# A hybrid decoder layer on one core: FFN's first tile with VectorE in program order, row scaling as a step of its own, block differences ahead of low parts

## The chip, the cores and the metric

The kernel runs on one core of a Trainium2 chip. The metric is the device time of one execution in microseconds (us), as the median of several runs. A profile of one more execution was taken; its times are counted from the start of its span.

## The reference, cut to what matters

The layer is `h = h + mixer(h)`, `h = h + cross_attention(h)`, `h = h + conv_glu(rmsnorm(h))`, with 1024 rows of 1024 columns. The change lies where the second line ends and the third begins:

```python
def conv_glu(hn, w_ffn_in, conv_w, conv_b, w_ffn_out):
    a, gate = jnp.split(hn @ w_ffn_in, 2, axis=-1)          # D_FF = 2816 columns each
    conv = conv_b + sum(a_pad[:, j:j + S] * conv_w[j] for j in range(3))
    return (jax.nn.gelu(conv) * gate) @ w_ffn_out
# hn = h * rsqrt(mean(h * h) + EPS) * g_ffn, row by row
```

## The kernel before, in words

Every f32 operand of a product is kept as a high and a low part (`xh`, `xl` or two halves of a page `wp`), and `mm3` (L308 to L311) makes each product of three matmuls. ScalarE (ACT) or GpSimd (POOL) rounds the high part, VectorE (DVE) or POOL subtracts for the low part.

**Rows.** The 1024 rows are eight groups `t` of 128, here called rows. `xo_unit(c, t)` computes half `c` of the output of cross attention for row `t`: 24 matmuls into one of two `acc` banks, then one addition on DVE (L1300) into `h2[t]`. After the second half, `f_norm(t)` stores `h2[t]` (a DMA issued by ACT, L1307), squares and sums it on ACT (L1135), makes the reciprocal root with two small DVE instructions (L133, L134) and ten small ACT instructions (L137), and scales the row with two DVE instructions of 128x512 (L1315), in place for rows 4 to 7. `f_tr(t)` transposes the scaled row on TensorE (PE, eight 128x128 transposes, L1381, into the two `trp` banks).

**The seven products.** `ffn_in(f)` computes one of 22 column tiles of the first FFN product for all rows with seven block products instead of eight (Strassen's scheme in Winograd's form): the operands are the blocks B11, B21, B22 and the sums T1 to T4 of the rows, and sums of the weights. For rows 0 to 3 `f_tr` splits the transposed row into B11 and B21 (ACT casts L1332, DVE low parts L1335). For rows 4 to 7 it makes B22 in the same way, x11 and x21 (L1346, on DVE and POOL), T1 = block - x11 (L1394, DVE), T2 = block - T1 (L1396, DVE), and with T2 on POOL T3 (L1398) and T4 (L1400). `xb_finish` splits each T of all four rows into high (ACT, L1360) and low parts (DVE, L1361). `product` issues 12 matmuls into one of six PSUM banks; DVE adds up the seven results (L1455). Then come the convolution (ACT L1496, DVE L1497 and L1498), the gelu (ACT L1499) and the gate (POOL L1504).

**Weights.** A queue of jobs loads and splits the weight pages. For each tile f there are the jobs A (2 pages), S (three DVE sums, L225 to L227), B (2 pages and the DVE difference L233), C (2 pages) and D (1 page). A page costs an ACT cast (L201) and a DVE subtraction (L204). `W.pump(1)` emits the next job if no more than 12 pages would be in use; a product gives its page back. The raw weights come by SP's queue into two buffers of 512 KB; a load is issued when the subtraction that read the buffer last is done.

**Order.** The program is traced once; a scheduler orders each engine's instructions from a model of their times. In the block `manual_schedule` (L1605 to L1618) PE keeps program order. Instructions of the program behind the block (tiles f = 1 to 21) may stand among those of the block on every engine.

Of the kernel before, what the change touches and what calls it, by code (L numbers as in the profile page):

```python
# [21 lines left out]
NT = 8  # L22
# [22 lines left out]
def hybrid_layer(ctx, tc, I, out):  # L45
# [28 lines left out]
    def trp():  # L74
        return ps.tile([P, 512], F32, name=nm("trp"), tag="tr", bufs=2)

    def accp():
        return ps.tile([P, 512], F32, name=nm("acc"), tag="acc", bufs=2)

    def small(name, shape=(P, 8), bufs=8):  # L80
        return wpool.tile(list(shape), F32, name=nm(name), tag=name, bufs=bufs)
# [47 lines left out]
    def rstd1(r, ss, scale):  # L129

        w = small("rst", (P, 3, 8), 4)
        m, y, t, u = (w[:, 0, j:j + 1] for j in range(4))
        dve.tensor_scalar(m, ss, scale, EPS, op0=OP.mult, op1=OP.add)  # L133
        dve.tensor_scalar(y.bitcast(I32), m.bitcast(I32), -0.5, 1597463007.0, op0=OP.mult, op1=OP.add)  # L134

        def mul(o, x, f, bias=0.0):
            act.activation(o, x, AF.Copy, bias=bias, scale=f)  # L137
        mul(t, y, y)
        mul(t, t, m)
        mul(t, t, -3.0 / 16, 9.0 / 16)  # L140
        mul(y, y, t)
        mul(t, y, y)
        mul(t, t, m)
        mul(u, t, 64.0 / 9, -10.0 / 3)
        mul(t, t, u)
        mul(t, t, 64.0 / 9, 5.0)
        mul(r, t, y)
# [16 lines left out]
    class Weights:  # L164
# [27 lines left out]
        def page(self, key):  # L192
            pg = wp()
            self.used += 1
            self.pages.setdefault(key, []).append(pg)
            return pg
# [79 lines left out]
    W = Weights()  # L276
# [31 lines left out]
    def mm3(o, lh, ll, rh, rl, start, stop):  # L308
        pe.matmul(o, lhsT=lh, rhs=rh, start=start, stop=False)  # L309
        pe.matmul(o, lhsT=lh, rhs=rl, start=False, stop=False)  # L310
        pe.matmul(o, lhsT=ll, rhs=rh, start=False, stop=stop)  # L311
# [782 lines left out]
    for s in range(-2, NA + 3):  # L1094
# [21 lines left out]
        u = s - 2  # L1116
# [16 lines left out]
    def norm_rows(src, jk, ssq, r):  # L1133

        act.activation(jk, src, AF.Square, accum_out=ssq)  # L1135
        rstd1(r, ssq, 1.0 / D)
# [47 lines left out]
    def w2(shape, dt, name):  # L1184
        return w2_at[0].tile(shape, dt, name=nm(name), tag="w2", bufs=w2_at[1])
# [101 lines left out]
    hf, hst = {}, {}  # L1287

    def xo_unit(c, t, mid=None):
        pages = W.get(("xo", c), 8)  # L1290
        half, u = divmod(t, 4)
        p = accp()
        for k in range(KT):
            oh, ol = ox[k // 4, (k % 4) // 2, half]
            s = slice(u * P, (u + 1) * P)
            if k == 4 and mid:
                mid()
            mm3(p, oh[:, k % 2, s], ol[:, k % 2, s], pages[k][:, 0, :], pages[k][:, 1, :], k == 0, k == KT - 1)
        hs = h2[t][:, c * 512:(c + 1) * 512]
        dve.tensor_tensor(hs, p, hs, op=OP.add)  # L1300
        if t == NT - 1:
            W.free(8)
        W.pump(1)

    def f_norm(t):
        rs = slice(t * P, (t + 1) * P)
        act.dma_start(h2_d[rs, :], h2[t])  # L1307
        st = small("st", (P, 12), 6)
        ws = [w2([P, 512], F32, "hn") for _ in range(1 if t >= 4 else 2)]
        norm_rows(h2[t], ws[0].bitcast(BF), st[:, 0:1], st[:, 1:2])  # L1310
        hn = []
        for g in range(2):
            hg = h2[t][:, g * 512:(g + 1) * 512]
            w = hg if t >= 4 else ws[g]
            dve.scalar_tensor_tensor(w, hg, st[:, 1:2], gff[g], op0=OP.mult, op1=OP.mult)  # L1315
            hn.append(w)
        hst[t] = hn
# [5 lines left out]
    def xb_new(name):  # L1323
        XB[name] = [[page([P, 2, 512], F32R, name) for _ in range(2)] for _ in range(2)]

    def xb_put(name, u, src, eh, el):
        ss = slice(u * P, (u + 1) * P)
        for v in range(2):
            hh, ll = (XB[name][i][v][:, :, ss] for i in range(2))
            x = src[:, 256 * v:256 * v + 256].rearrange("p (k q) -> p k q", k=2)  # L1330
            if eh == "a":
                act.copy(hh, x)  # L1332
            else:
                pool.tensor_scalar(hh, x, 1.0, 1.0, op0=OP.mult, op1=OP.mult)
            (dve if el == "d" else pool).tensor_tensor(ll, x, hh.bitcast(F32), op=OP.subtract)  # L1335

    def two(ap):
        return ap.rearrange("p (k q) -> p k q", k=2)

    def xb_sum(name, u, eng):  # L1340

        w = w2([P, 512], F32, "xf")
        ss = slice(u * P, (u + 1) * P)
        for v in range(2):
            hh, ll = (XB[name][i][v][:, :, ss].bitcast(F32) for i in range(2))
            eng.tensor_tensor(two(w[:, 256 * v:256 * v + 256]), hh, ll, op=OP.add)  # L1346
        return w

    def xb_finish(name):

        if name == "T4":
            xb_new(name)
            for u in range(4):
                xb_put(name, u, t4s[u], "a", "d")
            return
        XB[name] = [[], []]
        for v in range(2):
            f = tf[name][v]
            hh, ll = (page([P, 2, 512], F32R, name) for _ in range(2))
            act.copy(hh, f)  # L1360
            dve.tensor_tensor(ll, f, hh.bitcast(F32), op=OP.subtract)  # L1361
            XB[name][0].append(hh)
            XB[name][1].append(ll)
# [3 lines left out]
    def f_tr(t):  # L1367
        half, u = divmod(t, 4)
        if t == 0:
            xb_new("B11")  # L1370
            xb_new("B21")
        if t == 4:
            xb_new("B22")
            for n in ("T1", "T2", "T3"):
                tf[n] = [page([P, 2, 512], F32, n) for _ in range(2)]
        hn = hst.pop(t)
        ps_ = []
        for g in range(2):
            p = trp()
            for j in range(4):  # L1380
                pe.transpose(p[:, j * P:(j + 1) * P], hn[g][:, j * P:(j + 1) * P], ident)  # L1381
            ps_.append(p)
            if half == 0:
                xb_put(("B11", "B21")[g], u, p, "a", "d")
        if half == 0:
            return
        x11, x21 = xb_sum("B11", u, dve), xb_sum("B21", u, pool)
        ss = slice(u * P, (u + 1) * P)
        t1, t2, t3 = ([tf[n][v][:, :, ss] for v in range(2)] for n in ("T1", "T2", "T3"))
        t4s.append(x21)  # L1390
        vs = [slice(0, 256), slice(256, 512)]
        xb_put("B22", u, ps_[1], "a", "d")
        for v in range(2):
            dve.tensor_tensor(t1[v], two(ps_[0][:, vs[v]]), two(x11[:, vs[v]]), op=OP.subtract)  # L1394
        for v in range(2):
            dve.tensor_tensor(t2[v], two(ps_[1][:, vs[v]]), t1[v], op=OP.subtract)  # L1396
        for v in range(2):
            pool.tensor_tensor(t3[v], t2[v], two(x11[:, vs[v]]), op=OP.subtract)  # L1398
        for v in range(2):
            pool.tensor_tensor(two(x21[:, vs[v]]), two(x21[:, vs[v]]), t2[v], op=OP.subtract)  # L1400

    NU = 16
    for s in range(NU + 4):
        if s < NU:
            if s + 1 < NT:
                x_tr(s + 1, page)
            x_q(s)
            W.pump(1)
            if s == 1:
                x_kv()  # L1410
        if 0 <= s - 1 < NU:
            x_qt(s - 1)
        if 0 <= s - 2 < NU:
            x_s(s - 2)
        if 0 <= s - 3 < NU:
            x_pt(s - 3)
        if s + 3 < NT:
            x_norm(s + 3, w2([P, D], BF, "jk"))
        if s >= 4 and (s - 4) % 4 == 3:
            x_o((s - 4) // 8, ((s - 4) // 4) % 2)  # L1420
        if s >= NU - 1:
            for t in range(2 * (s - NU + 1), min(NT, 2 * (s - NU + 2))):
                h2.append((page if t < 4 else kq)([P, D], F32, "h2"))
                sp.dma_start(h2[t], h_d[t * P:(t + 1) * P, :])
        if s >= NU:
            xo_unit(0, s - NU)
        W.pump(1)
# [5 lines left out]
    for t in range(4, NT):  # L1433
        xo_unit(0, t)
# [167 lines left out]
        dve.tensor_tensor(lo, raw, hi.bitcast(F32), op=OP.subtract)  # L1602
        fo_pg[n] = (hi, lo)

    with tc.manual_schedule(engines={mybir.EngineType.PE}):  # L1605
        for t in range(NT):
            xo_unit(1, t, (lambda: f_tr(t - 2)) if t >= 2 else None)
            f_norm(t)
        first = ffn_in(0)
        next(first)  # L1610
        f_tr(6)
        next(first)
        f_tr(7)
        next(first)
        for n in ("T1", "T2", "T3", "T4"):
            xb_finish(n)
        for _ in first:
            pass  # L1618
# [119 lines left out]
```

## Time and profile before

| what | value |
|---|---|
| median of 3 runs | 1679.46 us (1676.55 to 1684.43) |
| the profiled execution | 1680.37 us, its span 1678.6 us |
| PE busy over the span | 1567.5 us (93%) |
| DVE busy | 1287.5 us (77%) |
| ACT busy | 771.2 us (46%) |
| POOL busy | 669.7 us (40%) |
| the block L1605 to L1618 in this execution | about 954 to 1055 us |
| tiles f = 1 to 21 | about 1055 to 1480 us |

A busy share is a mean over stages with different limits, so the windows of a stage count for more than this table. "PEclk" is the granted TensorE clock as a share of 2.4 GHz. In a timeline a row gives the start, the time from the first to the last of its merged instructions, engine, line, operation, output and inputs, the count, and in brackets how long the engine was idle before it and what ended that.

### The profile page before, as it was taken

How to read it: one execution, taken by the hardware profiler on the slowest of the kernel's cores; microseconds unless marked ns; L12 is line 12 of the kernel's file. 1: busy time of each engine (PE TensorE's matmuls, PEld its weight loads, DVE VectorE, ACT ScalarE, POOL GpSimd, SP SyncE). 2: the span in 40 equal slices, each digit the busy share in tenths (PEclk: the TensorE clock that was granted, in tenths of full speed). 3: DMA queues.
4: the chain of work that ended last, by engine and by line, in shares of the span. 5: the costliest groups of instructions: out<-in, count | busy, mean ns of one | idle time of the engine just before them, and what ended most of it. 6: DMA issues, size and time to landing. Idle time of an engine off the chain costs nothing.

```text
span 1678.6 us, 22444 instructions
## 1 busy us (share of the span) xinstructions
PE 1567.5 (93%) x7660; PEld 1283.1 (76%) x7660; DVE 1287.5 (77%) x2412; ACT 771.2 (46%) x1629; POOL 669.7 (40%) x908
## 2 busy tenths in 40 slices
PE   8899988878888998999999997999999999999999
PEld 7788766667777777977777775888887777788887
DVE  5736998998999988356645369998999999865554
ACT  6545577566656325527443165333333333343432
POOL 2736657535540122031101013557666666551121
PEclk9999999899989999999999998999999999999999
DMA  8321234212230122153303021455555555799812
GB/s 281 101 83 44 79 101 156 81 50 88 85 110 14 59 87 76 45 177 112 101 1 113 32 82 63 170 178 176 185 189 175 183 185 184 248 357 352 314 50 76
DMA packets 112162, 220.06 MB, mean 131 GB/s; under 512 B 18480, under 2 KB 38448, under 8 KB 112048
## 3 DMA queue, kind: packets, MB, share of 16 engines
q1 hardware_dynamic: 91072, 148.37, 26.6%
q0 software_dynamic: 18384, 61.36, 10.4%
q10 hardware_dynamic: 2592, 8.91, 1.4%
q8 instruction: 60, 0.98, 0.2%
q14 instruction: 54, 0.44, 0.1%
HBM read 160.92 MB, written 57.67 MB: 130 GB/s over the span
## 4 chain that ended last, share of the span: by engine, by line
PE 40%; DVE 37%; DMA 9%; issue 5%; ACT 4%; POOL 4%; ACTq 0%; SPq 0%; DVEq 0%; POOLq 0%
PE acc L309 7%; PE acc L310 7%; PE acc L311 7%; DVE jk L566 6%; DVE wp L204 5%; DMA raw<-in_w_ffn_in_dram 3%; PE big L309 2%; PE big L310 2%; PE big L311 2%; DMA fs<-u_d 2%; PE big L1277 2%; DVE fc L1497 2%; DVE fc L1498 2%; DVE e L775 2%; POOL fs L1551 2%
## 5 line engine op out<-in xcount | busy, mean ns | idle before, releaser
L204 DVE TENSOR_TENSOR wp<-raw,wp 128x512 fp32r<-128x512 f32 (+1 forms) x200 | 197.6, 997 | 23.8 <-ACT wp L201 15.2
L201 ACT CAST wp<-raw 128x512 fp32r<-128x512 f32 (+1 forms) x188 | 110.5, 614 | 173.6 <-DVE raw L227 119.5
L1602 DVE TENSOR_TENSOR wp<-fo,wp 128x1024 fp32r<-128x1024 f32 x77 | 105.5, 1386 | 76.0 <-ACT wp L1601 72.8
L1551 POOL TENSOR_TENSOR fs<-fs,fs 128x512 f32<-128x512 f32 x88 | 128.9, 1465 | 61.3 <-DMA fs<-u_d 48.5
L1601 ACT CAST wp<-fo 128x1024 fp32r<-128x1024 f32 x77 | 79.8, 1049 | 107.4 <-PE big L311 48.7
L309 PE MATMUL acc<-wp,xh 128*128 128x512 f32 (+1 forms) x272 | 110.5, 408 | 10.0 <-ACT X L647 10.0
L203 POOL TENSOR_SCALAR wp<-raw 128x512 fp32r<-128x512 f32 (+1 forms) x64 | 47.1, 749 | 179.1 <-DVE rst L110 63.5
L310 PE MATMUL acc<-wp,xh 128*128 128x512 f32 (+1 forms) x272 | 109.6, 404 | 0.0
L311 PE MATMUL acc<-wp,xl 128*128 128x512 f32 (+1 forms) x272 | 109.3, 402 | 0.0
L683 ACT COPY pt<-trp 128x512 f32<-128x512 f32 (+3 forms) x144 | 65.8, 477 | 67.6 <-PE trp L692 67.0
L204 POOL TENSOR_TENSOR wp<-raw,wp 128x512 fp32r<-128x512 f32 x52 | 69.3, 1350 | 45.6 <-ACT wp L201 45.6
L1038 PEld LDWEIGHTS acc<-va_t,pt 128*128 128x128 f32 x576 | 74.0, 195 | 7.0 <-ACT pt L683 4.9
L1038 PE MATMUL acc<-va_t,pt 128*128 128x65 f32 x576 | 76.6, 273 | 2.4 <-ACT pt L683 1.9
L1083 POOL DMA_DIRECT2D h_d<-xr x16 | 9.4, 586 | 168.5 <-DVE xr L1082 150.1
L1648 POOL TENSOR_TENSOR hr<-hr,r 128x512 f32<-128x512 f32 x16 | 26.3, 1657 | 115.4 <-DMA fo<-u_d 56.9
L1021 ACT ACTIVATE ea<-ea,sta 128x128 f32<-128x128 f32 (+7 forms) x64 | 49.3, 777 | 49.9 <-DVE sta L1020 46.6
L309 PEld LDWEIGHTS acc<-wp,xh 128*128 128x128 f32 x272 | 52.7, 194 | 23.6 <-ACT X L647 12.2
L566 DVE TENSOR_SCALAR_CACHE_REDUCE jk<-mb,cx 128x640 bf16<-128x640 uint16 (+1 forms) x64 | 68.6, 1072 | 0.7
L566 DVE TENSOR_SCALAR_CACHE_REDUCE jk<-mb,cand 128x640 bf16<-128x640 bf16 (+3 forms) x60 | 64.3, 1072 | 0.4
L310 PE MATMUL acc<-wp,wp 128*128 128x512 f32 x152 | 61.0, 401 | 2.6 <-DVE wp L204 2.6
L1499 ACT ACTIVATE fc<-fc 128x1024 f32<-128x1024 f32 x22 | 23.4, 1062 | 86.5 <-DVE fc L1498 86.5
L777 ACT ACTIVATE e<-e,st 128x1024 f32<-128x1024 f32 (+7 forms) x64 | 49.4, 774 | 27.9 <-DVE st L775 27.8
(423 smaller groups left out, 5161.1 us busy)
## 6 DMA issues: line engine op xcount, KB each, us to landing
raw<-in_w_ffn_in_dram SPq DMA_DIRECT2D x44, 512.0 KB, 4.2
fs<-in_w_ffn_out_dram POOLq DMA_DIRECT2D x44, 256.0 KB, 3.7
ws_d<-fs POOLq DMA_DIRECT2D x44, 256.0 KB, 2.3
fs<-u_d POOLq DMA_DIRECT2D x44, 256.0 KB, 3.8
us_d<-fs POOLq DMA_DIRECT2D x44, 256.0 KB, 2.8
fo<-us_d SPq DMA_DIRECT2D x44, 256.0 KB, 5.3
fo<-ws_d SPq DMA_DIRECT2D x44, 256.0 KB, 5.4
u_d<-fg POOLq DMA_DIRECT2D x21, 512.0 KB, 4.1
```

What stands on the lines that cost most here:

```text
L201: act.copy(pg[:, 0, :n], src)
L204: (dve if el == "d" else pool).tensor_tensor(pg[:, 1, :n], src, pg[:, 0, :n].bitcast(F32), op=OP.subtract)
L309: pe.matmul(o, lhsT=lh, rhs=rh, start=start, stop=False)
L310: pe.matmul(o, lhsT=lh, rhs=rl, start=False, stop=False)
L311: pe.matmul(o, lhsT=ll, rhs=rh, start=False, stop=stop)
L566: dve.tensor_scalar(jk[:, :n], src, th[:, j:j + 1], None, op0=OP.is_ge, op1=OP.add, accum_out=cnt[:, j:j + 1])
L683: act.copy(dst, src)
L777: last["act"] = act.activation(e[:, :n], e[:, :n], AF.Exp, bias=st[:, c:c + 1], scale=-1.0, accum_out=st[:, 4 + c:5 + c])
L1038: pe.matmul(acc[:, hh * 65:hh * 65 + 65], lhsT=pt, rhs=va_t[:, kt, :], start=kt == 0, stop=kt == i)
L1551: pool.tensor_tensor(o, p, q, op=op)
L1601: act.copy(hi, raw)
L1602: dve.tensor_tensor(lo, raw, hi.bitcast(F32), op=OP.subtract)
```

## The change

DVE is put in program order inside the block as PE is. The two scaling instructions leave `f_norm` for a function `f_scale`, which for row t is called in the middle of row t+1 (behind `f_tr(t-1)`, ahead of the addition of row t+1), for row 7 behind `f_tr(6)`. In `f_tr` of rows 4 to 7 the low parts of B22 go behind T1 and T2. The pump in `xo_unit(1, 7)` (job C of f = 0) moves behind `f_scale(7)` and the second product. T2 is finished ahead of T1.

```diff
         if t == NT - 1:
             W.free(8)
-        W.pump(1)
+        if c == 0 or t < NT - 1:
+            W.pump(1)
...
         norm_rows(h2[t], ws[0].bitcast(BF), st[:, 0:1], st[:, 1:2])
+        hst[t] = (st, ws)
+
+    def f_scale(t):
+
+        st, ws = hst.pop(t)
         hn = []
...
-        xb_put("B22", u, ps_[1], "a", "d")
         for v in range(2):
             dve.tensor_tensor(t1[v], two(ps_[0][:, vs[v]]), two(x11[:, vs[v]]), op=OP.subtract)
         for v in range(2):
             dve.tensor_tensor(t2[v], two(ps_[1][:, vs[v]]), t1[v], op=OP.subtract)
+        xb_put("B22", u, ps_[1], "a", "d")
...
-    with tc.manual_schedule(engines={mybir.EngineType.PE}):
+    with tc.manual_schedule(engines={mybir.EngineType.PE, mybir.EngineType.DVE}):
         for t in range(NT):
-            xo_unit(1, t, (lambda: f_tr(t - 2)) if t >= 2 else None)
+            def mid():
+                if t >= 2:
+                    f_tr(t - 2)
+                if t >= 1:
+                    f_scale(t - 1)
+            xo_unit(1, t, mid)
             f_norm(t)
         first = ffn_in(0)
         next(first)
         f_tr(6)
+        f_scale(7)
         next(first)
+        W.pump(1)
         f_tr(7)
         next(first)
-        for n in ("T1", "T2", "T3", "T4"):
+        for n in ("T2", "T1", "T3", "T4"):
             xb_finish(n)
```

## Rows read from the trace of the kernel before

**Rows 1.** Busy time by stretch: us, PE, PEld, DVE, ACT, POOL, PEclk, DMA, GB/s.

```profile
...
954.00:1009.00 55.00, 53.64 (x257) 43.67 (x255) 37.98 (x79) 32.88 (x104) 7.19 (x8) 1.00 0.25 95
1009.00:1019.00 10.00, 0.89 (x5) 0.89 (x5) 9.80 (x15) 6.34 (x23) 7.57 (x8) 0.71 0.32 111
1019.00:1055.00 36.00, 33.44 (x139) 26.25 (x138) 35.07 (x56) 19.21 (x34) 7.46 (x8) 0.94 0.22 72
...
1160.00:1260.00 100.00, 100.00 (x431) 80.56 (x430) 92.75 (x97) 32.54 (x50) 65.98 (x70) 1.00 0.52 178
1260.00:1490.00 230.00, 223.50 (x944) 177.38 (x943) 206.74 (x212) 76.96 (x108) 140.59 (x151) 0.99 0.60 208
```

**Rows 2.** Timeline of PE, the block.

```profile
969.79 1.29 PE L1381 MATMUL trp<-ident,hn 128*128 128x128 f32 x8 [1.02 <-DVE hn L1315]
...
1001.95 0.60 PE L1381 MATMUL trp<-ident,h 128*128 128x128 f32 x4
...
1018.14 1.94 PE L1381 MATMUL trp<-ident,h 128*128 128x128 f32 x8 [9.11 <-issue]
...
1027.20 0.39 PE L309 MATMUL trp<-B,wp 128*128 128x512 f32 x1
...
1036.93 0.50 PE L310 MATMUL big<-T,wp 128*128 128x512 f32 x1 [1.18 <-DVE T L1361]
```

**Rows 3.** Timeline of DVE, rows 0, 3 and 4.

```profile
963.03 0.68 DVE L1300 TENSOR_TENSOR h<-acc,h 128x512 f32<-128x512 f32 x1
...
968.89 1.41 DVE L1315 SCALAR_TENSOR_TENSOR hn<-h,st,gff 128x512 f32<-128x512 f32 x2 [2.14 <-ACT st L137]
...
980.25 0.69 DVE L1300 TENSOR_TENSOR h<-acc,h 128x512 f32<-128x512 f32 x1 [1.05 <-PE acc L311]
...
986.63 0.69 DVE L1300 TENSOR_TENSOR h<-acc,h 128x512 f32<-128x512 f32 x1 [1.05 <-PE acc L311]
```

**Rows 4.** Timeline of ACT, the last small instruction of row 3.

```profile
986.48 0.29 ACT L137 ACTIVATE st<-rst 128x1 f32<-128x1 f32 x1
```

**Rows 5.** Timeline of DVE, scalings and low parts.

```profile
1000.34 2.36 DVE L1315 SCALAR_TENSOR_TENSOR h<-h,st,gff 128x512 f32<-128x512 f32 x2
...
1017.30 1.40 DVE L1315 SCALAR_TENSOR_TENSOR h<-h,st,gff 128x512 f32<-128x512 f32 x2
...
1028.30 2.56 DVE L1361 TENSOR_TENSOR T<-T,T 128x1024 fp32r<-128x1024 f32 x2
...
1045.16 1.42 DVE L1335 TENSOR_TENSOR T<-xf,T 128x256 fp32r<-128x256 f32 x4
```

**Rows 6.** Timeline of POOL, row 4.

```profile
1000.96 1.19 POOL L1398 TENSOR_TENSOR T<-T,xf 128x256 f32<-128x256 f32 x1
```

**Rows 7.** Groups of DVE, 1009 to 1054.85 us: count, busy, mean ns, idle before.

```profile
L204 DVE TENSOR_TENSOR wp<-raw,wp 128x512 fp32r<-128x512 f32 x13 | 10.8, 838 | 0.9 <-ACT wp L201 0.9
...
L226 DVE TENSOR_TENSOR raw<-raw,raw 128x512 f32<-128x512 f32 x2 | 2.4, 1216 | 0.0
...
L204 DVE TENSOR_TENSOR wp<-ws,wp 128x512 fp32r<-128x512 f32 x2 | 1.4, 676 | 0.0
```

**Rows 8.** All waits of DVE from 1060 to 1460 us: total, times, longest.

```profile
DVE fc L1497 <- ACT fc L1496: 12.0, 17, 1.4
DVE ws L225 <- DMA raw<-in_w_ffn_in_dram: 11.2, 17, 2.1
DVE wp L204 <- ACT wp L201: 5.9, 12, 0.5
DVE wp L1602 <- ACT wp L1601: 3.4, 2, 2.1
```

**Rows 9.** Timeline of PE, a wait late in the FFN.

```profile
1469.51 0.50 PE L309 MATMUL acc<-wp 128*128 128x512 f32 x1 [1.93 <-DVE fg L1455]
```

**Rows 10.** Busy time by stretch, behind that wait.

```profile
1472.00:1474.00 2.00, 2.00 (x6) 1.51 (x6) 0.82 (x2) 1.06 (x1) 1.13 (x2) 0.50 0.62 183
```

**Rows 11.** Loads of raw weights, the page's DMA issues.

```profile
raw<-in_w_ffn_in_dram SPq DMA_DIRECT2D x44, 512.0 KB, 4.2
```

## The prediction

> **What bounds the kernel now.** I read the windows by stage first, then the timelines of the block, then the waits behind it. The block has two faces [rows 1]. To 1009 us PE is full, and DVE is busy for 38 of 55 us. From 1009 to 1055 it is the other way round: PE works 0.9 of the first 10 us and 33.4 of the next 36, and DVE 9.8 and 35.1. In the tiles behind it PE has no idle time from 1160 to 1260, and from 1260 to 1490 it lacks 230 - 223.5 = 6.5 us, while DVE is busy for about 92% throughout. The timeline of PE shows the gaps [rows 2]: 1.02 us ahead of the transposes of row 0, 9.11 us ahead of those of row 6, 1.18 us in product T2, and behind the long gap a lower granted clock (0.71 for the stretch [rows 1]; eight transposes take 1.94 us where those of row 0 took 1.29).
>
> What was DVE doing in the 9 us? Not the scaling that PE waited for, which ran at 1017.30 [rows 5]. From 1009 to 1054.85 it made 15 page subtractions and two each of the three sums and the difference of jobs S and B (the row of L226 stands for these four lines): 15 + 8 = 23 instructions of weight splits for tiles f = 1 and up, before tile 0 was done [rows 7]. That is work that has to be done anyhow. And from 1060 to 1460 DVE waits 32.5 us in all, for ACT and for weight loads and never for PE [rows 8]: there it sets its own pace. So PE's gap is what one sees, but DVE's work is what reaches the end, and DVE had no idle time to give in the gap.
>
> **The change part by part.**
>
> Scaling a step later. In program order DVE now goes: root of row t (two instructions), low parts of row t-1, scaling of row t, addition of row t+1. The addition starts the next row's squares, so a loop closes that was open before, when the addition went ahead of the scaling. From an addition to its scaling it takes 968.89 - 963.03 = 5.86 us in row 0 [rows 3], and 986.48 + 0.29 - 980.25 = 6.52 us to the end of the last small instruction in row 3, where four casts lie among ACT's ten [rows 3, 4]. The pair of scalings adds 1.41 us. The loop takes 7.27 to 7.93 us; a row on PE takes 986.63 - 980.25 = 6.38 us. I take 7.3: the transposes can start 969.79 - 968.89 = 0.90 us into the scaling, so most casts fall where ACT waits for the addition. Behind DVE's wait for the root stand the low parts, and PE waits for the scaled row.
>
> Row 0's addition no longer stands behind splits: PE was done with it at about 960.4 us (968.77, where the transposes of row 0 would have begun, less one and a half units of 24 matmuls at 0.232 us, from 431 in 100 us [rows 1]), and it ran at 963.03. So the transposes of row 5 come at 960.4 + 0.2 + 5 x 7.3 + 5.86 + 0.90 = 1003.9 us, before at 1001.95 [rows 2]: 1.9 us later (1000.9 to 1007.0 for loops of 6.38 to 7.93).
>
> The gap. From row 4 on POOL's differences, which follow T2, run beside the scaling: a pair took 2.36 us beside POOL and 1.40 alone [rows 5, 6]. I take 7.8 us for a loop there, between 7.3 and 8.3. The transposes of row 6 come at 1011.7 (PE is ready at 1003.9 + 0.9 + 2.8 + 2.8 = 1010.4, a product being 12 x 0.232 = 2.8), 6.4 us earlier than 1018.14. What is late next is the transposes of row 7, one loop later at 1019.5, though PE is done with product B21 at 1015.4: a wait of 4.1 us. Then B22: from the scaling of row 7 at 1018.6 DVE has 1.4 + 0.6 (an addition) + 1.2 (job C) + 8 x 0.355 [rows 5] = 6.0 us of work ahead of its last low part, so B22 starts at 1024.7, a wait of 4.3 us. Low parts behind the differences put B22 back by four instructions, 1.4 us of this, and give T2 0.7 us that nobody waits for. The price of the lower clock after such waits I take from a wait of 1.93 us late in the FFN, behind which two us ran at 0.50 [rows 9, 10]: 1 us lost for certain; I take 2 for the two waits, between 0 and 4.
>
> To the end of tile 0. T2 ahead of T1 does away with the 1.18 us. The finishing on DVE takes 6 x 1.28 + 8 x 0.355 = 10.5 us [rows 5], to 1035.2, the addition that frees T3's bank stands behind it, and T3 starts at 1035.9, a wait of 0.8 us. From there PE has work (T3, the first products of f = 1, T4). At 1055 PE has done 11.8 products; before it was 2 and (1055 - 1027.2 - 1.2) / 2.78 = 9.6 [rows 2], 11.6. So the gap that goes comes back as three smaller ones: PE is even, with 5 us either way.
>
> The moved pump. Job C is two casts, two subtractions and one load of 512 KB on SP's queue, which lands 4.2 us after its issue [rows 11]. C ends near 1022, its load lands at 1026 and is wanted at 1037: hidden. D's load lands near 1041, when S of f = 1 is due: DVE may wait up to 1 us, with two additions of tile 0 and L1497 behind it.
>
> What DVE has not done by then. In program order only A, S and B of f = 1 lie inside the block, 8 instructions against 23. Tile 0's L1498 ends at about 1049.5 instead of 1054.8; in the 5.5 us to 1055 DVE can make 4 or 5 splits. It is 10 or 11 instructions behind and 3 additions of f = 1 ahead: 7 at 0.838 us (mean of the thirteen [rows 7]) are 6 us. Nearest bounds: 0, if they go into the 32.5 us of waits [rows 8]; 11 at 1.216 us = 13 [rows 7], if nothing is made up. I take 6, as DVE has never waited for PE there, and PE's 6.5 us show that its lead was used up.
>
> **Sum**, against the profiled execution of 1680.37 us (span 1678.6 and 1.8 around it): PE 0, DVE +6, and the later one counts: 1686.4. The median of the runs is 0.9 below that execution: 1685.5 us.
>
> **One rule of the skill.** A scaling pair beside POOL took 0.96 us longer than alone [rows 5]. The Trainium skill, SBUF — State Buffer, section "Who interferes with whom", says that a VectorE instruction with two SBUF inputs and a GpSimd instruction that reads SBUF exclude each other for their whole length. By that rule a pair can lose two whole instructions of POOL, and the sum would be 11 us in place of 6. The trace shows less than half of that for this pair.
>
> **Rivals.** Faster: PE decides after all. If the casts and small instructions fit so well that the loop keeps PE's 6.38 us, the transposes of row 5 come at 1000.9, everything behind them 3 us earlier, two waits shrink by 1.4 each and the half clock goes (2 us): 8 to 9 us, about 1671. It decides once the loop is under 6.4 us and the missing splits fit into DVE's waits. For it speaks PE at 100% to 1260; against it 5.86 + 1.41 us with no cast among them. Slower by the lost lead: all 11 splits at 1.0 to 1.2 us, with every later tile as slow as now: +11 to +13, 1691; for it speak [rows 8]. Slower by the loop beside POOL: if each scaling of a pair waits for one whole instruction of POOL, 1.19 us [rows 6], a loop takes 7.3 + 2.4 = 9.7 us, and 1.9 more in three loops add 5 to 6 us to the 6: 1690. It decides if POOL's differences start ahead of both scalings; against it, the pair seen lost 0.96 us. Nothing happens: instructions from behind the block may stand among it, as product `trp<-B` of f = 1 did at 1027.20 among those of tile 0 [rows 2]; if the scheduler so fills DVE's gaps with splits, the lead stays: 1679.5.
>
> **How the numbers follow.** A measurement of this kernel can tell about 0.5%, 8.4 us, from no change. Within it lie the forecast (0.40) and nothing happens (0.14): 0.54. Slower by more: lost lead 0.20, loop beside POOL 0.12: 0.32. Faster: 0.14. The range 1671 to 1697 goes from the faster rival to the upper bound of 13 us with 4 more for the clock. The forecast's own range is 1675 to 1688.
>
> **What would show it.** Right: additions of rows 3 to 7 over 7 us apart, waits of 3 to 5 us ahead of the transposes of row 7 and of B22, none of 9 us; fewer than 12 split instructions of f = 1 and up before L1498 of tile 0; more than 6.5 us of idle PE from 1260 to 1490. Wrong: additions 6.4 us apart, or PE waits in the later tiles that don't grow.

## The result and the profile after

The changed kernel is slower: 1703.22 us in the median of 4 runs (1701.99 to 1703.71), the kernel before 1679.52 us beside it (4 runs, 1676.55 to 1684.43); the ratio is 1.0124, 95% interval [1.011, 1.0138], which is some 21 us; the two medians are 23.7 us apart (1.4%). The time lies above the predicted range. The profiled execution took 1703.43 us, its span 1701.7 us, 23.1 us more than before.

Where do the 23.1 us lie? I cut both spans at three events: the addition of `xo_unit(0, 4)` (L1300, at 943.02 us before and 946.48 us after; up to there every engine's order is the same in both), the first convolution step of tile 0 on DVE (L1497 before, L1503 after) and that of tile 3. Windows by stage of the kernel before, between these events (columns as in [rows 1]):

```profile
943.02:1050.70 107.68, 94.10 (x424) 75.74 (x424) 83.97 (x150) 57.06 (x157) 25.60 (x28) 0.95 0.20 72
1050.70:1104.51 53.81, 53.81 (x232) 43.38 (x231) 48.35 (x59) 19.92 (x29) 30.34 (x32) 1.00 0.51 175
```

The same of the changed kernel:

```profile
946.48:1060.32 113.84, 98.57 (x429) 77.55 (x429) 71.47 (x138) 53.05 (x149) 25.56 (x33) 0.94 0.18 68
1060.32:1126.85 66.53, 63.85 (x271) 50.30 (x270) 60.16 (x71) 24.24 (x38) 34.15 (x34) 1.00 0.46 158
```

The first stretch is 6.2 us longer, the second 12.7: 18.9 of the 23.1 us. Another 3.5 us lie ahead of the first event and are not the change's (a second profile of the kernel before, below, has that event 3.7 us later too); the last 0.7 us lie behind tile 3. The third number to read is DVE's busy time: 83.97 + 48.35 = 132.3 us before, 71.47 + 60.16 = 131.6 us after. The windows hold the same number of DVE instructions too, 150 + 59 and 138 + 71. **DVE does the same work between the first event and the last; what grew is its idle time,** from 161.5 - 132.3 = 29.2 to 180.4 - 131.6 = 48.7 us. PE, in contrast, waits 2.7 us in the whole second stretch.

Nearly all the new idle time, 18.7 of 19.5 us, lies in the first stretch (23.7 us before, 42.4 after). One third of it makes that stretch 6.2 us longer; the rest, 12.5 us, is work that is not done there (71.47 us in place of 83.97) and goes over into the second. The waits of DVE in the first stretch name it. Before:

```profile
DVE h L1300 <- PE acc L311: 13.2, 8, 5.3
DVE B L1335 <- ACT B L1332: 5.8, 8, 1.1
DVE hn L1315 <- ACT st L137: 2.1, 1, 2.1
DVE rst L133 <- ACT hn L1135: 1.8, 4, 1.0
```

After:

```profile
DVE h L1300 <- PE acc L311: 14.0, 4, 5.3
DVE B L1341 <- ACT B L1338: 11.6, 16, 1.7
DVE rst L133 <- ACT hn L1135: 8.3, 6, 1.6
DVE hn L1321 <- ACT st L137: 5.7, 4, 3.0
DVE fg L1461 <- PE big L311: 2.2, 2, 1.4
```

Low parts wait for their casts (+5.8), the root for the squares (+6.5), the scaling for the last small instruction (+3.6 in this line). Most of these waits are 0.5 to 1.6 us long, and in program order DVE has nothing else to put there. Before, the scheduler had put weight splits between the instructions of the block. Since the first event DVE had made 37 split instructions (L204, L225 to L227, L233) when tile 0's convolution began; the changed kernel 24. It makes the other 13 between tile 0 and tile 3. Splits made ahead of their tile are called the lead below. Groups of DVE from 1050.70 to 1104.51 us before (count, busy, mean ns):

```profile
L204 DVE TENSOR_TENSOR wp<-raw,wp 128x512 fp32r<-128x512 f32 x16 | 15.1, 947 | 1.4 <-ACT wp L201 1.4
L225 DVE TENSOR_TENSOR ws<-raw 128x512 f32<-128x512 f32 x3 | 3.7, 1234 | 0.3 <-DMA raw<-in_w_ffn_in_dram 0.3
L233 DVE TENSOR_TENSOR raw<-raw 128x512 f32<-128x512 f32 x3 | 3.1, 1018 | 0.1
```

and from 1060.32 to 1126.85 us after:

```profile
L204 DVE TENSOR_TENSOR wp<-raw,wp 128x512 fp32r<-128x512 f32 x23 | 20.4, 906 | 1.0 <-ACT wp L201 1.0
L233 DVE TENSOR_TENSOR raw<-raw 128x512 f32<-128x512 f32 x5 | 5.6, 1118 | 0.0
L225 DVE TENSOR_TENSOR ws<-raw 128x512 f32<-128x512 f32 x4 | 3.7, 929 | 3.2 <-DMA raw<-in_w_ffn_in_dram 3.2
```

With L226, L227 and the page from `ws` it is 31 instructions before and 44 after (one in each was already running when the window began); 12.7 us for 13 is 0.98 us each. This quotient is not yet a price of one split; the runs that put splits back are below.

Two windows by stage, those of [rows 1] shifted by 3.46 us, show DVE's share in the rows and in the old gap: 30.6 of 55 us (before 37.98), 5.92 of 10 (before 9.80), while PE, at 0.89 before, is busy for 9.79:

```profile
957.46:1012.46 55.00, 49.57 (x232) 39.41 (x231) 30.60 (x66) 30.82 (x97) 5.63 (x8) 0.99 0.20 77
1012.46:1022.46 10.00, 9.79 (x43) 7.81 (x42) 5.92 (x16) 5.84 (x18) 5.18 (x6) 0.89 0.25 98
```

Inside the block the timeline of PE answers to [rows 2] (subtract 3.46 us to compare):

```profile
979.18 1.29 PE L1387 MATMUL trp<-ident,hn 128*128 128x128 f32 x8 [0.54 <-DVE hn L1321]
...
1011.13 1.89 PE L1387 MATMUL trp<-ident,h 128*128 128x128 f32 x8 [2.89 <-issue]
...
1027.57 0.63 PE L1387 MATMUL trp<-ident,h 128*128 128x128 f32 x4 [3.98 <-issue]
...
1033.48 0.80 PE L309 MATMUL big<-B,wp 128*128 128x512 f32 x1 [3.64 <-ACT B L1338]
1046.26 0.47 PE L309 MATMUL big<-T,wp 128*128 128x512 f32 x1 [0.89 <-DVE u L1461]
```

The gap of 9.11 us is gone; in its place stand 2.89 us ahead of row 5, 3.98 ahead of row 7, 3.64 ahead of B22, and PE is idle in the whole first stretch for 113.84 - 98.57 = 15.3 us, before for 13.6. The wait ahead of B22 ends with a cast on ACT, and the timeline of ACT shows what that cast stood behind: in ACT's order the finishing cast of T2 came first, and it waited for DVE's last T2.

```profile
1032.11 1.04 ACT L1366 CAST T<-T 128x1024 fp32r<-128x1024 f32 x1 [6.13 <-DVE T L1401]
1033.06 0.36 ACT L1338 CAST B<-trp 128x256 fp32r<-128x256 f32 x1
```

The timeline of DVE from row 5's addition to row 6's answers to [rows 3]:

```profile
1001.87 0.68 DVE L1300 TENSOR_TENSOR h<-acc,h 128x512 f32<-128x512 f32 x1
1004.14 0.15 DVE L133 TENSOR_SCALAR rst<-st 128x1 f32<-128x1 f32 x1 [1.59 <-ACT hn L1135]
...
1007.88 0.42 DVE L1341 TENSOR_TENSOR B<-trp,B 128x256 fp32r<-128x256 f32 x1 [1.41 <-ACT B L1338]
...
1009.71 1.99 DVE L1321 SCALAR_TENSOR_TENSOR h<-h,st,gff 128x512 f32<-128x512 f32 x2 [0.33 <-ACT st L137]
1011.62 0.68 DVE L1300 TENSOR_TENSOR h<-acc,h 128x512 f32<-128x512 f32 x1
```

This is the closed loop: root, low parts, scaling, and only then the next addition, 9.75 us here. The additions of rows 0 to 7 are 6.99, 8.58, 7.5, 7.38, 7.38, 9.75 and 8.17 us apart. In the longest loop the scaling comes 7.84 us after the addition, in the loop before 6.05; ACT has three weight casts among its small instructions, the first of them after a wait of 0.56 us:

```profile
1006.25 0.62 ACT L201 CAST wp<-raw 128x512 fp32r<-128x512 f32 x1 [0.56 <-PE acc L311]
...
1006.98 0.60 ACT L201 CAST wp<-raw 128x512 fp32r<-128x512 f32 x1
...
1007.95 0.60 ACT L201 CAST wp<-raw 128x512 fp32r<-128x512 f32 x1
...
1009.38 0.30 ACT L137 ACTIVATE st<-rst 128x1 f32<-128x1 f32 x1
```

The later tiles run as before, with more waiting: DVE's waits from 1063.46 to 1463.46 us, which answer to [rows 8], and the window that answers to the last of [rows 1].

```profile
DVE ws L225 <- DMA raw<-in_w_ffn_in_dram: 26.8, 15, 3.6
DVE fc L1503 <- ACT fc L1502: 10.2, 14, 0.8
```

```profile
1263.46:1512.00 248.54, 236.19 (x999) 187.28 (x998) 206.69 (x222) 82.14 (x115) 153.59 (x161) 0.99 0.59 205
```

From tile 3's step to tile 21's the two kernels take the same time, and there idle time of DVE is not what counts. Before, then after:

```profile
1104.51:1467.57 363.06, 358.49 (x1527) 285.87 (x1526) 330.34 (x346) 117.60 (x175) 234.44 (x249) 1.00 0.55 189
1126.85:1490.16 363.31, 349.49 (x1483) 276.60 (x1481) 309.17 (x346) 116.86 (x174) 229.88 (x244) 1.00 0.55 188
```

DVE is idle for 54.1 us in place of 32.7, and as many instructions (346) are busy for 21 us less; 99 page subtractions alone (L204) take 108.4 us in place of 116.4. A busy time of DVE is no fixed amount of work, so the account by idle time is shown for the two stretches alone. What sets the pace of the later tiles stays open.

### The profile page after: what moved, and what is told of

Read it like the earlier page. It is cut to its first block, busy times and chain, and to the rows that moved or that the text cites. A ratio compares the mean times of both kernels' runs of the same rounds, so it can differ in the third digit from the quotient of the medians.

```text
span 1701.7 us, 22466 instructions
## 1 busy us (share of the span) xinstructions
PE 1574.5 (93%) x7660; PEld 1284.3 (75%) x7660; DVE 1264.9 (74%) x2412; ACT 770.8 (45%) x1629; POOL 668.8 (39%) x908
## 4 chain that ended last, share of the span: by engine, by line
PE 41%; DVE 35%; DMA 9%; ACT 5%; issue 5%; POOL 3%; ACTq 0%; DVEq 0%; POOLq 0%; SPq 0%
PE acc L309 7%; PE acc L310 7%; PE acc L311 7%; DVE wp L204 6%; DVE jk L566 5%; DMA raw<-in_w_ffn_in_dram 4%; PE big L309 2%; PE big L310 2%; PE big L311 2%; DVE fc L1504 2%; DVE fc L1503 2%; PE big L1277 2%; DVE e L775 2%; PE acc L1038 2%; DVE ea L1020 1%
## 5 line engine op out<-in xcount | busy, mean ns | idle before, releaser
L204 DVE TENSOR_TENSOR wp<-raw,wp 128x512 fp32r<-128x512 f32 (+1 forms) x200 | 187.2, 947 | 21.6 <-ACT wp L201 13.3
L1608 DVE TENSOR_TENSOR wp<-fo,wp 128x1024 fp32r<-128x1024 f32 x77 | 102.0, 1340 | 76.0 <-ACT wp L1607 73.5
L1557 POOL TENSOR_TENSOR fs<-fs,fs 128x512 f32<-128x512 f32 x88 | 130.0, 1477 | 68.2 <-DMA fs<-u_d 45.0
L1607 ACT CAST wp<-fo 128x1024 fp32r<-128x1024 f32 x77 | 79.8, 1049 | 108.3 <-PE big L311 48.7
L204 POOL TENSOR_TENSOR wp<-raw,wp 128x512 fp32r<-128x512 f32 x52 | 69.4, 1353 | 45.6 <-ACT wp L201 45.6
L1510 POOL TENSOR_TENSOR fg<-fc,fg 128x1024 f32<-128x1024 f32 x21 | 51.4, 2446 | 32.6 <-ACT fc L1505 32.5
```

Source lines behind the costliest of these rows:

```text
L204: (dve if el == "d" else pool).tensor_tensor(pg[:, 1, :n], src, pg[:, 0, :n].bitcast(F32), op=OP.subtract)
L1510: pool.tensor_tensor(g, cv, g, op=OP.mult)
L1557: pool.tensor_tensor(o, p, q, op=op)
L1607: act.copy(hi, raw)
```

## The experiments

In the table "to 0" is the time from the first event to tile 0's convolution step, "0 to 3" from there to tile 3's, both from each kernel's one profile; "idle" is the sum of both less DVE's busy time in them, and "splits" the split instructions made before tile 0's step (not given for e6 and e7, where POOL makes a part of them). The ratio is against the kernel before on the same chip. The expected times were set against its 1679.5 us; beside the experiments it took 1681 to 1685 us, so that they are compared by the ratio.

| kernel | ratio [95%] | to 0 | 0 to 3 | idle | splits |
|---|---|---|---|---|---|
| before | 1 | 107.7 | 53.8 | 29.2 | 37 |
| after | 1.0124 [1.011, 1.0138] | 113.8 | 66.5 | 48.7 | 24 |
| e1_dve_free | 1.0054 [1.0038, 1.0069] | 105.8 | 58.3 | 35.7 | 35 |
| e2_order_alone | 1.0216 [1.0188, 1.0243] | 130.8 | 66.6 | 65.2 | 24 |
| e3_open_loop | 1.0073 [1.005, 1.0095] | 106.9 | 64.0 | 39.1 | 24 |
| e4_rows_only | 1.0100 [1.0076, 1.0124] | 115.2 | 57.8 | 44.5 | 36 |
| e5_tile_only | 1.0086 [1.0059, 1.0112] | 107.7 | 63.4 | 40.2 | 24 |
| e6_pool_lows_after | 1.0122 [1.0099, 1.0144] | 112.4 | 71.2 | 54.4 | |
| e7_pool_lows_before | 1.0079 [1.005, 1.0107] | 107.7 | 58.3 | 32.3 | |
| e8_diffs_first | 1.0064 [1.0041, 1.0088] | 105.4 | 58.4 | 33.2 | 35 |
| e9_pump_alone | 0.9991 [0.9977, 1.0006] | 107.5 | 55.0 | 29.3 | 37 |
| e10_lows_alone | 1.0105 [1.0084, 1.0127] | 111.7 | 58.4 | 39.6 | 36 |
| e11_t2_first_alone | 1.0012 [0.9997, 1.0027] | 107.4 | 54.7 | 29.2 | 37 |
| e12_after_old_b22 | 1.0127 [1.0106, 1.0149] | 112.6 | 66.8 | 46.3 | 24 |
| e13_rows_open_tile_free | 1.0086 [1.0066, 1.0106] | 111.1 | 58.6 | 39.2 | 36 |
| e14_rows_open_old_b22 | 1.0089 [1.0063, 1.0115] | 112.0 | 55.8 | 33.9 | 37 |
| e15_splits_back | 1.0101 [1.0081, 1.0121] | 118.4 | 60.1 | 49.2 | 31 |
| e16_splits_back_open_loop | 1.0063 [1.0045, 1.0082] | 110.7 | 59.9 | 41.7 | 31 |

In all eighteen rows DVE's busy time in the two stretches lies between 128.5 and 133.8 us, while the stretches together go from 161.5 to 197.4. In sixteen of them the work is the same; in e6 and e7 a part of it went to POOL.

**Which part of the program order.** e1 takes DVE out of the manual order again and keeps the other edits.

```diff
-    with tc.manual_schedule(engines={mybir.EngineType.PE, mybir.EngineType.DVE}):
+    with tc.manual_schedule(engines={mybir.EngineType.PE}):
```

> The changed kernel with VectorE given back to the scheduler in the block; the later scaling, the moved pump, the differences ahead of low parts and T2 first stay. Theory 'order' (program order makes VectorE wait and leaves splits of later tiles undone, and its work sets the end): the time is back within 0.5% of before, 1671 to 1688 us, and 18 or more split instructions of later tiles stand ahead of tile 0's end again. Rival 'placement' (the scaling behind the differences and the low parts behind T2 cost, whoever orders them): 1695 to 1705 us.

By the ratio the time lies just above the range of theory 'order'. More than half of the loss goes (1.0124 to 1.0054), and 11 of the 13 splits are back. The program order is the larger part; a rest of about 9 us stays, of which the profile has 2.7 us in the two stretches (164.2 us for 161.5) and 4.1 behind tile 3.

e2 is the kernel before with DVE in program order and no other edit.

> The kernel before with VectorE in program order in the block and nothing else changed: the scaling waits for the root right behind it, and the low parts of the row before come after it. Theory 'order': the loop from addition to addition grows by the low parts that no longer lie beside ACT's small instructions, 7.3 to 9 or 10 us, and the time is above the changed kernel's, 1708 to 1725 us. Rival 'placement': with the old places of the scaling and the low parts it is no slower than the changed kernel, 1690 to 1703 us.

1.0216, about 15 us above the changed kernel (0.92% of 1680). From row 1 on its additions stand 9.4 to 13.5 us apart, since scaling, low parts and addition all follow in one chain. So the scaling as a step of its own, with the other edits, is worth these 15 us; it repairs most of what program order costs, not all.

e4 ends DVE's program order ahead of tile 0 (the line below), e5 gives it to tile 0 alone.

```diff
+    with tc.manual_schedule(engines={mybir.EngineType.PE}):
         first = ffn_in(0)
```

> The changed kernel with VectorE in program order for the eight rows only; tile 0 (behind row 7) is left to the scheduler. Theory 'order, lost lead' (most of the loss is the splits that are not made beside tile 0): the lead comes back, 1683 to 1692 us. Rival 'loop of rows' (the loop of addition and scaling costs most): 1697 to 1704 us.

> The changed kernel with the eight rows left to the scheduler on VectorE and program order only from tile 0 on. Theory 'order, lost lead': most of the loss stays, 1690 to 1699 us, with additions of the rows 6.4 us apart. Rival 'loop of rows': the loss goes, 1677 to 1686 us.

By the ratio e4 comes to 1696 us, 4 us above its theory's range and at the edge of its rival's, and e5 to 1694, in its theory's: neither loss is the whole. e4 has the splits (36) and the short way from tile 0 to 3 (57.8 us), but comes to tile 0 7.5 us late. e5 comes to tile 0 in time (107.7), 13 splits short, and pays 9.6 us up to tile 3. **The rows lose time ahead of tile 0; tile 0 loses the lead.** They part the two losses in the main and not cleanly: to row 6 e4's additions stand as in the changed kernel, but row 7's comes 13.8 us behind row 6's (8.2 there), with ten splits between the two.

e3 keeps everything in program order and puts the scaling behind the addition.

```diff
             xo_unit(1, t, mid)
+            if t >= 1:
+                f_scale(t - 1)
             f_norm(t)
```

(the two lines leave `mid`).

> The changed kernel with the scaling of row t behind the addition of row t+1 (rows 0 to 6) in place of ahead of it; VectorE stays in program order. Theory 'loop' (the scaling ahead of the addition makes rows 7.0 to 9.8 us apart): additions 6.4 to 6.6 us apart in rows 2 to 4, the block shorter by 4 to 7 us, 1696 to 1700 us. Rival 'lead alone' (rows matter little, since VectorE's missing splits set the rest): 1701 to 1705 us.

The additions of rows 2 to 6 are 7.4 and then three times 6.4 us apart, the latter as PE makes them, tile 0 comes at 106.9 us, and the way to tile 3 stays at 64.0. Opening the loop brings 113.8 - 106.9 = 6.9 us, all that tile 0 was late, and leaves the lead as it was. Its windows, where the second stretch is still long and full of DVE's work, also settle which engine counts: in the first stretch PE is idle for only 9.3 us, less than the 13.6 of the kernel before, and yet 10.2 us are lost behind it. PE's gaps don't make this loss. By the ratio the time is 1692 us, 4 us less than expected.

```profile
946.98:1053.85 106.87, 97.60 (x435) 77.90 (x435) 73.68 (x137) 53.18 (x149) 27.89 (x34) 0.95 0.21 74
1053.85:1117.85 64.00, 62.14 (x265) 49.17 (x264) 58.06 (x72) 25.26 (x39) 32.70 (x32) 1.00 0.47 161
```

**Moving splits off DVE.** e6 and e7 give the low parts of the pages of f = 1 and 2 to POOL, in the changed kernel and in the kernel before.

```diff
+        FIW = ("a", "p") if f in (1, 2) else ("a", "d")
```

> The changed kernel with the low parts of the weight pages of tiles 1 and 2 made by GpSimd in place of VectorE: 14 subtractions taken away from VectorE, nothing else. Theory 'lead' (splits that VectorE has not made in the block are paid one by one between tile 0 and tile 3, at 0.8 to 1.0 us): the time from tile 0's L1503 to tile 3's falls from 66.5 to 54 to 58 us, and the whole is 1690 to 1695 us. Rival 'gaps of PE' (PE's waits in the block set the loss): 1700 to 1706 us.

> The kernel before with the low parts of tiles 1 and 2 made by GpSimd. Theory 'VectorE sets the end': VectorE has up to 14 subtractions less from 1009 us on, and the kernel gets faster by 5 to 9 us, 1672 to 1676 us. Rival (PE sets the end, VectorE's work is hidden) 1679 to 1683 us; slower if GpSimd's subtractions at 1.35 us come too late for PE.

Both theories failed: e6 is where the changed kernel is, e7 is slower than before. POOL's subtractions of a page take 1.35 us each, and PE now waits for one of them. Groups of POOL, and waits of PE, in e6 from 1059 to 1130.3 us:

```profile
L204 POOL TENSOR_TENSOR wp<-raw,wp 128x512 fp32r<-128x512 f32 x9 | 11.8, 1345 | 0.0
```

```profile
PE big L312 <- POOL wp L204: 3.3, 1, 3.3
```

DVE gains nothing either: in e7 it makes 14 subtractions fewer between the events and is busy for 133.7 us (132.3 before), since others of its instructions got longer (16 scalings 15.2 us for 12.2, six low parts of T 10.7 for 7.9). So these two runs say nothing of the lead; they show that POOL is no free place for it.

**The other edits.** e8 is the kernel before with the differences ahead of B22's low parts and T2 ahead of T1; e10 and e11 have one of the two each, e9 has job C's moved pump alone.

> The kernel before with the block differences ahead of the low parts and T2 finished first; VectorE free, scaling and pump in their old places. With VectorE free all edits but the order cost 9 us. If these two placements are the cause: 1686 to 1691 us; if the later scaling or the moved pump is: 1678 to 1683 us.

> The kernel before with one edit, job C's pump behind the second product. If that edit is harmless, as the prediction took it, the ratio is within 0.3% of 1. If moving one job changes the order in which weights are split and so costs in the tiles behind the block, 1.003 to 1.006.

> The kernel before with B22's low parts behind the differences, T1 still finished ahead of T2. If the loss of e8_diffs_first (0.6%) comes from late low parts of B22 in the block, all of it is here: 1.005 to 1.007, and tile 0 ends over 3 us later than before. If it comes from VectorE's order in the later tiles, where e8 makes a page's low part ahead of the second sum in most tiles and this kernel does not, 1.000 to 1.003.

> The kernel before with T2 finished ahead of T1 and nothing else. VectorE's order differs from before in tiles 0 to 2 alone. If the loss needs the low parts or the later tiles' order: within 0.2% of 1. If T2 ahead of T1 alone costs the 0.6% of e8: 1.005 to 1.007.

In the kernel before, the moved pump and T2 ahead of T1 are free. Late low parts of B22 are not free where the scheduler orders DVE: 1.0105, against both sizes expected. Of its loss the profile has 8.6 us in the two stretches and 6.4 behind tile 3. The timeline of DVE shows a cause for the former: the last low part of B22 goes not only behind the differences but behind five finishings of T too.

```profile
1030.59 3.33 DVE L1361 TENSOR_TENSOR T<-T,T 128x1024 fp32r<-128x1024 f32 x2
1033.85 0.41 DVE L1335 TENSOR_TENSOR B<-trp,B 128x256 fp32r<-128x256 f32 x1
...
1038.40 1.21 DVE L1361 TENSOR_TENSOR T<-T,T 128x1024 fp32r<-128x1024 f32 x1
1039.53 0.41 DVE L1335 TENSOR_TENSOR B<-trp,B 128x256 fp32r<-128x256 f32 x1
```

and PE stands in the middle of B22:

```profile
1040.00 0.80 PE L310 MATMUL big<-B,wp 128*128 128x512 f32 x1 [4.03 <-DVE B L1335]
```

With T2 first as well (e8) that wait is 2.32 us and the ratio 1.0064.

e12 puts both edits back in the changed kernel.

> The changed kernel with B22's low parts ahead of the differences and T1 ahead of T2, as before. If the costs of the parts add up, about 0.6% under the changed kernel, a ratio of 1.005 to 1.007 against before. If with VectorE in program order these two edits cost nothing, or gain as meant, the ratio stays at 1.011 to 1.015.

The time doesn't change (1.0127), though tile 0 comes 1.2 us earlier: where the program orders DVE, the low parts can't slip behind the finishings. The parts of the change don't add up; the price of this one depends on who orders DVE.

**Splits put back.** e15 emits jobs earlier within program order, e16 does so in e3.

```diff
             xo_unit(1, t, mid)
+            if t == NT - 1:
+                W.pump(2)
             f_norm(t)
...
             xb_finish(n)
+            if n in ("T2", "T1"):
+                W.pump(1)
```

> The changed kernel with jobs C and D of f = 0 emitted ahead of row 7's norm, A of f = 1 behind the second product and S and B behind the first two finishings: some nine more splits before tile 0's first convolution step (33 in place of 24). If missing splits cost what they take later, tiles 0 to 3 are 7 to 9 us closer together, and the ratio is about 1.007 (1.004 to 1.010). If the splits are not the cause, 1.011 to 1.015 as the changed kernel.

> e15 with the scaling behind the addition (e3's edit). If the two losses add up, 6 us less than e15: a ratio of 1.001 to 1.006. If the loop's gain is swallowed because VectorE is the bound anyway, as e15.

Seven splits more before tile 0 (31 for 24; nine were expected) shorten the way to tile 3 by 66.5 - 60.1 = 6.4 us, 0.92 us each: here, with DVE still in program order, a missing split costs what it takes later. But e15 comes to tile 0 4.6 us later: the three splits take 2.43 us ahead of row 7's root, its scaling comes 2.4 us later after the first event, and PE waits 6.01 us for its transposes, where it waited 3.98. DVE's idle time hardly changes (49.2 us), and so the gain is small: 1.0101 lies between the two expected ranges. In e16 the loop's gain comes on top: its median is 7.9 us under e15's, 6 were expected (1.0063, just above its range).

**Loop open, tile 0 free.** e13 is e3's and e4's edits together, e14 has the old B22 and T order besides.

> The changed kernel with the scaling behind the addition and VectorE in program order for the rows alone. If closed loop and missing splits are the whole loss, only what e10 showed for late low parts is left: 1.004 to 1.010 against before, 35 or more splits before tile 0's first convolution step. If the program order of the rows costs by itself, 1.010 or more, as e4.

> e13 with B22's low parts ahead of the differences and T1 ahead of T2, as before. If closed loop, missing splits and late low parts are all, the ratio is 0.997 to 1.003. If the rows' program order costs by itself, 1.005 or more.

e13's time fell where late low parts alone would put it. e14 did not come back to 1 as expected if loop, lead and low parts were all: it is 4.3 us late at tile 0, 1.9 in the next stretch, and its profile has 9 us more behind tile 3. So loop, lead and late low parts are not all. Its timelines show where the 4.3 us arise. From row 3's addition to row 6's its additions are 6.4 to 6.7 us apart, but row 7's comes 14.2 us behind row 6's (8.4 in the kernel before):

```profile
1005.09 0.68 DVE L1300 TENSOR_TENSOR h<-acc,h 128x512 f32<-128x512 f32 x1
...
1019.25 0.68 DVE L1300 TENSOR_TENSOR h<-acc,h 128x512 f32<-128x512 f32 x1
```

Between the two the scheduler has put seven splits, and the root, the low parts and row 7's addition stand behind them in their fixed order. PE waits twice for a scaled row, where the kernel before has the one gap of 9.11 us:

```profile
1021.13 2.26 PE L1387 MATMUL trp<-ident,h 128*128 128x128 f32 x8 [7.21 <-issue]
...
1034.24 2.27 PE L1387 MATMUL trp<-ident,h 128*128 128x128 f32 x8 [6.76 <-issue]
```

e13 has six splits at this place, the two additions 13.2 us apart and waits of 5.47 and 5.53 us, so that its agreement with late low parts is in part chance. The splits came back, but in front of the rows.

These kernels also bound the price of a split. From e3 to e13 twelve splits more shorten the way from tile 0 to tile 3 by 5.4 us, from the changed kernel to e4 by 8.7 us, in e15 seven by 6.4: 0.45 to 0.92 us each. And with 35 to 37 splits ahead of tile 0, e1, e4, e8, e10, e13 and e14 still need 55.8 to 58.6 us for this way, the kernel before 53.8. So the number of splits explains the greater part of the 12.7 us, and some 2 to 5 us of them stay open.

**The same kernels again.**

> The kernel before without any edit, for a second profile. If the place of the block in the span (first addition at 943.0 us) and the time behind tile 3 differ by chance, they differ here too, by up to 4 us ahead of the block; if they belong to the kernel, they come back within 1 us.

> The changed kernel without any edit, for a second profile. From the block's first addition to tile 3's first convolution step 179 to 182 us as in the first profile, with 47 to 50 us of them idle on VectorE. If the 3.5 us ahead of the block are chance, the first addition stands elsewhere than at 946.5 us; if they belong to the change, within 1 us of it.

The kernel before measured 0.9999 [0.9985, 1.0012] against itself, the changed kernel 1.0147 [1.0121, 1.0172]. Windows of the second profile of the kernel before:

```profile
946.72:1054.26 107.54, 93.25 (x424) 75.08 (x424) 84.19 (x150) 56.98 (x157) 25.58 (x28) 0.95 0.20 72
1054.26:1108.34 54.08, 54.08 (x233) 43.60 (x232) 48.65 (x58) 19.91 (x29) 30.21 (x32) 1.00 0.51 175
```

and of the changed kernel:

```profile
948.73:1062.56 113.83, 98.62 (x429) 77.56 (x429) 71.44 (x138) 53.03 (x149) 25.62 (x33) 0.94 0.19 68
1062.56:1127.95 65.39, 63.60 (x272) 50.40 (x271) 59.57 (x72) 25.21 (x39) 34.35 (x34) 1.00 0.47 161
```

The place of the first event moves by 3.7 us in the kernel before (943.02 and 946.72) and by 2.3 in the other: chance. The two stretches come back within 0.2 us (161.6) and 1.2 us (179.2). Behind tile 3 the same kernel differs by -1.9 and +3.6 us from its first profile. So the 17.6 to 18.9 us between the events belong to the change; of what the spans differ by behind tile 3, from -3 to +10 us over all kernels, the first 4 us are no evidence. What lies beyond (5 to 6 us in e3, e10, e12 and e13, 8 to 10 in e8, e14 and e7) goes with longer waits of DVE for raw weights (L225): in the 360 us behind tile 3 they are 11.0 us before, 11.7 in e9 and 11.3 in e16, but 27.0, 22.7 and 29.7 in e8, e14 and e7. The changed kernel, with 23.5, loses only 0.7 us there, so that this is a companion and no shown cause; it stays open.

## Why the prediction was wrong

The direction and the engine were right, the sum was not: 6 us were forecast; 21 came by the ratio, 23.7 by the medians, and 18.9 of them can be placed.

- **What bounds the kernel** was right for this loss: "PE's gap is what one sees, but DVE's work is what reaches the end". The plainest sign is e3, where PE is idle for 4.3 us less up to tile 0 and the kernel is still 0.73% slower. (One reading beside it was loose: DVE is busy for 93% from 1160 to 1260 us and 90% behind it, not "about 92% throughout".)
- **The loop.** Forecast 7.3 us; 7.57 in the mean of the five to row 5. Beside POOL 7.8 was forecast and 9.75 and 8.17 came. Of the 2.4 us that 9.75 lies above the loop before it, 1.8 arise ahead of the scaling, with the weight casts on ACT, and 0.6 in the pair beside POOL. The transposes of row 5 were forecast at 1003.9 and came at 1011.13 - 3.46 = 1007.7: 1.3 us of the 3.8 are the five loops, 2.0 the way from row 5's addition to its scaling (7.84 us for 5.86) with those casts, 0.5 the way from there to the transposes (1.42 for 0.90). The cast-free row 0 was the wrong row to take the chain from.
- **The waits of PE** were right in size: 4.1 us forecast ahead of row 7 and 3.98 measured, 4.3 ahead of B22 and 3.64, 0.8 for T3 and 0.89. For B22 that is luck: the forecast had DVE's low parts as its cause, and what ended it was ACT's cast, which stood behind the finishing cast of T2. Behind it the granted clock was 0.50 (1.2 GHz) from 1033.48 to 1038.50 us, 2.5 us lost, where the forecast took 2 for two waits. And all of it came late: the transposes of row 7 by 4.6 us, B22 by 5.3, T3 by 6.9 (1042.8 for 1035.9).
- **"PE is even, with 5 us either way"** failed by the same delay: at 1055 us (1058.46 in the changed kernel) PE had begun 9.7 products, 11.4 in the kernel before, and stood 4.9 us behind, at the edge of what the forecast allowed.
- **The step that failed is the DVE term, "I take 6".** It has two halves. The first is tile 0's end: forecast 1049.5 us, 5 us earlier than before; it came at 1064.25 + 1.27 - 3.46 = 1062.1. T3 was already 6.9 us late, and behind it DVE waits four times for PE, ACT or a load (0.83, 0.19, 1.13 and 1.42 us) and L1503 takes 2.81 us for 1.27. The sum priced DVE's instructions and treated the waits between them as if they could be filled; program order is just what forbids that. The second half is the lead: 10 or 11 splits behind, less 3 additions, were 7 at 0.838 = 6 us; it was 13 splits, and tile 3's step came 12.7 us later against tile 0's, with no credit for the additions and none from the 32.5 us of waits in the later tiles, which do not take splits that tiles 1 to 3 need now. That the upper bound of 13 us (11 at 1.216) meets 12.7 is chance: the count was too low, and the price by the runs that put splits back is 0.45 to 0.92 us, so that a part of the 12.7 us stays open.
- **"The later one counts"** failed with it: tile 0 late by 6.2 us and the lead of 12.7 us add up, since both come out of the 18.7 us of new idle time of the one engine. In DVE's waits nearly all of it can be read (+5.8, +6.5, +3.6 and smaller ones); the prediction named two of them, the root and the low parts, and gave them no price of their own.
- **The rivals.** Lost lead was the right mechanism for the longer stretch of 12.7 of the 18.9 us, and the closed loop for the rest (e3, e4, e5 part them in the main); the text held them for alternatives with chances of their own, and they came together. The loop rival's 9.7 us came (9.75), but not for its reason, POOL in front of both scalings. That the two are the whole is not shown: with both undone, e13 and e14 still need 8.2 and 6.3 us more than the kernel before in the two stretches, and their own new order of splits makes a part of that. The scheduler filling DVE's gaps with splits did not happen (24 splits).
- **The moved pump** at nothing was right in the kernel before (e9). T2 first did away with the wait of PE in T2 (none in the changed kernel, 1.48 us in e12), and no time follows from it (e11). Differences first were to put B22 back by 1.4 us; with DVE in program order e12, without them, reaches tile 0 1.2 us earlier in the same time, and where the scheduler orders DVE they cost 1% (e10).
- **What would show it**: additions over 7 us apart, two waits of 3 to 5 us, fewer than 12 splits of f = 1 and up (10), more idle PE late (248.5 - 236.2 = 12.4 us) all came. None of these signs measures the size.

## What to carry to other kernels

When an engine that is the bound is put in program order, add up its idle time, not only its work: in the two stretches here every wait for another engine that a scheduler used to fill with work from further on became time, partly as delay of the stretch and partly as work left for the next. Before closing an order, look for a loop (A waits for B, and the next A stands behind B) and compare its length with the period of the stage; here 7.4 to 9.8 us stood against 6.4, and putting the addition ahead of the scaling opened it. An edit priced at nothing holds for one way of ordering the engine alone.

## What the runs showed of the hardware

Scaling pairs beside POOL's sums and differences took 1.99, 1.89 and 2.45 us where a pair alone takes 1.41, and L1503 took 2.81 us for 1.27 beside a POOL instruction (L1557) of 1.31. The Trainium skill, SBUF — State Buffer, section "Who interferes with whom", has such instructions exclude each other for their whole length; with POOL's instructions at 0.73 us the pairs lost 0.5 to 1.0 us, less than two whole instructions, so the trace agrees that they collide and does not show that both scalings of a pair pay in full. Splits given to POOL (1.35 us, for 0.68 on DVE [rows 7]) made nothing faster (e6, e7). And one and the same kernel reached the block 3.7 us apart in two executions with the rest of the way to tile 3 equal within 0.2 us: a difference of single spans of that size says nothing before it is placed.
